# The weights' low parts kept in DRAM between the two token halves

## The chip, the cores and the metric

The kernel runs on one core of a Trainium2 chip. The engines are named as the profile names them: PE is TensorE (matmuls; PEld is its loading of weights), DVE is VectorE, ACT is ScalarE, POOL is GpSimd, and SP (SyncE) issues most DMAs. The metric is the device time of one execution in microseconds (us), the median of several runs.

## The reference

Two layers of a decoder trunk over 1024 tokens of width 1024, in float32. Each layer is

```python
a = rmsnorm(h, norm_mix_pre[i])
u = jnp.einsum('bsd,de->bse', a, w_in[i])
...
mix = jnp.concatenate([y_attn, y_conv, y_pool], axis=-1)
mix = jnp.einsum('bse,ed->bsd', mix, w_out[i])
h = h + rmsnorm(mix, norm_mix_post[i])
m = rmsnorm(h, norm_mlp_pre[i])
m = jnp.square(jax.nn.relu(jnp.einsum('bsd,df->bsf', m, w_up[i])))
m = jnp.einsum('bsf,fd->bsd', m, w_down[i])
h = h + rmsnorm(m, norm_mlp_post[i])
gate = jax.nn.sigmoid(jnp.einsum('bsd,de->bse', h, ple_gate[i]))
h = h + gate * jnp.einsum('bsp,pd->bsd', p[i], ple_proj[i])
```

`y_attn` is an attention in which an indexer picks 256 keys for each query, `y_conv` a causal convolution of 31 taps with a layer norm, `y_pool` a set of trailing means.

## The kernel before

The tokens are cut into two halves of 512. `PHASES` lists what is done in which order, for (layer, half): the input projections of both halves of layer 0, then the long phase "m" (output projection, MLP, gate) of half 0, then the input projection of layer 1 for half 0, and so on. So every weight matrix is used twice: by half 0, and some hundred microseconds later by half 1. The attention and the convolution of a half (`conv_pool`, `attention`) are generators that are advanced beside the dense work, with a budget per phase (`RATES`).

A **unit** is one output block of 128 columns for one token half: eight blocks of 128 rows of a weight matrix times eight slices of the input, into one PSUM bank. Matmuls run on a short float format, so weight and input are each split into a high and a low part, and a unit takes three matmuls for each of the eight blocks (`dense`): high x high, high x low (L248, or L246 where `fresh` is set) and low weight x high input (L249, or L245), 24 in all. A phase "m" has 8 output blocks, 4 half-size units for the layer's extra embedding, 32 up, 32 down and 8 gate units; an input projection has 21.

`prepare` brings the weights of one unit: SP loads the raw block of 512 KB into one of two buffers `wraw` (L199); for each half of it (four row blocks) ACT copies it into the short format, the high part `whi` (L204), and POOL subtracts this from the raw block, which gives the low part `wlo` (L205). `whi` and `wlo` have four half-size buffers each, so two units fit. `weights` calls `prepare` for the next unit just before the matmuls of the present one are written; each half buffer comes free when the matmuls of the half unit that read it are done. Semaphore waits follow from these buffers.

The instructions of each engine are then put in order by a scheduler that simulates the time: it may let matmuls of two or three units take turns where an operand comes late. This happens behind a normalisation (`post_norm`): the eight input slices of the next units are made one after another, by DVE (L867, L266 or L261), POOL (the addition L868) and ACT (L265), and PE has two units, with `fresh` set, work on each slice as it comes. I call such a place a joint.

Of the kernel before, what the change touches and what calls it, by code (L numbers as in the profile page):

```python
# [8 lines left out]
F32 = mybir.dt.float32  # L9
F32R = mybir.dt.float32r  # L10
# [6 lines left out]
OP = mybir.AluOpType  # L17

P = 128
S = 1024  # L20
D = 1024
DEPTH = 2
HALF = 512
NK = D // P
# [22 lines left out]
WIN_ORDER = WIN_ATT + WIN_CONV  # L47


def win_order(l, hf):  # L50

    return WIN_CONV + WIN_ATT if CONV_FIRST[l][hf] else WIN_ORDER
# [34 lines left out]
def tile_trunk(ctx: ExitStack, tc: tile.TileContext, xT, pT, pos, vecs, invf, cinv,  # L87
               win, wout, wup, wdown, wgate, wple, wcp, outT):
    nc = tc.nc
    te, ve, sc, gp, sy = nc.tensor, nc.vector, nc.scalar, nc.gpsimd, nc.sync  # L90
# [5 lines left out]
    dram = ctx.enter_context(tc.tile_pool(name="dram", bufs=1, space=bass.MemoryType.DRAM))  # L96
# [20 lines left out]
    cpS = dram.tile([DEPTH, 512, S], F32, name="cpS")  # L117
    eS = dram.tile([DEPTH, NK, P, S], F32, name="eS")
    tabS = dram.tile([4, P, S], F32, name="tabS")


    slots = Ring("slot", 16, [P, 2, HALF], F32R)
    wraw = Ring("wraw", 2, [P, 8, P])
    whi = Ring("whi", 4, [P, 4, P], F32R)
    wlo = Ring("wlo", 4, [P, 4, P], F32R)
    dtmp = Ring("dtmp", 11, [P, HALF])
    ctmp = Ring("ctmp", 5, [P, HALF])
    cmat = Ring("cmat", 6, [P, HALF], F32R)
# [64 lines left out]
        dtmp.put(*got)  # L193


    def prepare(src):
        n = src.shape[1] // 4
        raw = wraw.get()
        sy.dma_start(raw[:, :4 * n], src)  # L199
        parts = []  # L200
        for i in range(n):
            hi, lo = whi.get(), wlo.get()
            r = raw[:, 4 * i:4 * i + 4]
            sc.activation(hi, r, AF.Copy)  # L204
            gp.tensor_tensor(lo, r, hi.bitcast(F32), op=OP.subtract)  # L205
            parts.append((hi, lo))
        wraw.put(raw)
        return parts


    coming = []
    for l, hf, phase in PHASES:
        if phase == "win":
            coming += [win[l, WIN_ORDER.index(n)] for n in win_order(l, hf)]
        else:
            if (l, hf) == (0, 0):
                coming += [wout[l, o][:, 4:] for o in range(NK)] + [wout[l, o][:, :4] for o in range(NK)]
            else:
                coming += [wout[l, o] for o in range(NK)]
            coming += [wple[l, i] for i in range(2, 4)]  # L220
            for gr in range(4):
                coming += [wup[l, gr * 8 + u] for u in range(8)] + [wdown[l, gr, o] for o in range(NK)]
            coming += [wple[l, i] for i in range(2)] + [wgate[l, o] for o in range(NK)]
    ready = []

    def weights():
        while coming and (not ready or len(ready) <= 1 and len(whi.free) >= 2):
            ready.append(prepare(coming.pop(0)))
        return ready.pop(0)

    def done(parts):
        for hi, lo in parts:
            whi.put(hi)
            wlo.put(lo)

    def pieces(parts):
        return [(hi[:, j], lo[:, j]) for hi, lo in parts for j in range(4)]

    def dense(ps, ws, xs, fresh=False):

# [10 lines left out]
    def unit(xs, fresh=False):  # L251
        ws = weights()
        ps = pd.get()
        dense(ps, pieces(ws), [(x[:, 0], x[:, 1]) for x in xs], fresh)
        done(ws)
        return ps
# [6 lines left out]
    def split_g(hi, lo, src, g):  # L263

        sc.activation(hi, src, AF.Identity, scale=g)  # L265
        ve.scalar_tensor_tensor(lo, src, g, hi.bitcast(F32), op0=OP.mult, op1=OP.subtract)  # L266
# [617 lines left out]
    def embedding(l, hf, pairs, keep):  # L884

        ts = slice(hf * HALF, hf * HALF + HALF)
        pl = [slots.get() for _ in range(2)]
        for c in range(2):
            x = dtmp.get()
            sy.dma_start(x, pT[l, c * P:(c + 1) * P, ts])  # L890
            split(pl[c][:, 0], pl[c][:, 1], x)
            dtmp.put(x)

        def fill():
            for i in pairs:
                w = weights()
                for j in range(2):
                    pp = pd.get()
                    dense(pp, pieces(w)[2 * j:2 * j + 2], [(x[:, 0], x[:, 1]) for x in pl])
                    e = dtmp.get()  # L900
                    sc.activation(e, pp, AF.Copy, scale=0.5)
                    pd.put(pp)
                    if keep is not None:
                        keep.append(e)
                    else:
                        sy.dma_start(eS[l, 2 * i + j, :, ts], e)
                        dtmp.put(e)
                    yield
                done(w)
            slots.put(*pl)  # L910
        return fill
# [117 lines left out]
    def first_x(hf):  # L1029
        ts = slice(hf * HALF, hf * HALF + HALF)  # L1030
        sq = Sq()
        xs = []
        for k in range(NK):
            h = dtmp.get()
            sy.dma_start(h, xT[k * P:(k + 1) * P, ts])
            if k == 0 and hf == 0:
                ready.append(prepare(coming.pop(0)))
            x = slots.get()
            xs.append(x)
            split_g(x[:, 0], x[:, 1], h, vec[:, 0, V_MIX_PRE + k:V_MIX_PRE + k + 1])  # L1040
            sq.add(h)
            dtmp.put(h)
        return xs, sq
# [33 lines left out]
    def drain(l, hf):  # L1077

        while advance([x for x in bg if x[0] == (l, hf)]) is not None:
            pass  # L1080

    state["x", 0, 0] = first_x(0)
    for i, (l, hf, phase) in enumerate(PHASES):
        if phase == "win":
            extra = {}
            if i == 0:
                extra = {2: lambda: (sy.dma_start(fr, invf), rope_tables(0)), 5: lambda: rope_tables(1),
                         16: lambda: state.update({("x", 0, 1): first_x(1)})}
            run(win_phase(l, hf, *state["x", l, hf]), RATES[i], extra)
        else:  # L1090
            drain(l, hf)
            run(m_phase(l, hf), RATES[i])
# [62 lines left out]
```

## Time and profile before

| | us |
|---|---|
| median of three runs | 2885.41 |
| lowest and highest of them | 2882.80, 2891.74 |
| the profiled execution | 2882.24 |
| its span, first to last instruction | 2880.4 |

| engine | busy us | share of the span |
|---|---|---|
| PE | 2736.7 | 95% |
| DVE | 1917.1 | 67% |
| ACT | 1477.3 | 51% |
| POOL | 1468.7 | 51% |

The page gives the busy time of each engine; a view by phase gives the same for stretches of the span, with the TensorE clock that was granted (1.00 is full speed) and the share of time in which the 16 DMA engines moved packets. The views of waits say for each engine after whose instruction it went on. The order of time lists instructions with their start, their length and, in brackets, the idle time of the engine before them and what ended it. A matmul's row is 0.39 us long, but matmuls are pipelined and follow each other more closely; what counts is the distance of their starts. The phases, by their DMAs: input projections of layer 0 from 0 to 150 us (half 0) and to 300 us (half 1); phase "m" of half 0 to 930 us; input projection of layer 1, half 0, to 1190 us (with the gate before it); phase "m" of layer 0, half 1, to 1650 us; input projection of layer 1, half 1, to 1800 us; the phases "m" of layer 1 to 2376 and 2880 us.

### The profile page before, as it was taken

How to read it: one execution, taken by the hardware profiler on the slowest of the kernel's cores; microseconds unless marked ns; L12 is line 12 of the kernel's file. 1: busy time of each engine (PE TensorE's matmuls, PEld its weight loads, DVE VectorE, ACT ScalarE, POOL GpSimd, SP SyncE). 2: the span in 40 equal slices, each digit the busy share in tenths (PEclk: the TensorE clock that was granted, in tenths of full speed). 3: DMA queues.
4: the chain of work that ended last, by engine and by line, in shares of the span. 5: the costliest groups of instructions: out<-in, count | busy, mean ns of one | idle time of the engine just before them, and what ended most of it. 6: DMA issues, size and time to landing. Idle time of an engine off the chain costs nothing.

```text
span 2880.4 us, 37724 instructions
## 1 busy us (share of the span) xinstructions
PE 2736.7 (95%) x12648; PEld 2250.3 (78%) x12648; DVE 1917.1 (67%) x3473; ACT 1477.3 (51%) x2804; POOL 1468.7 (51%) x1161
## 2 busy tenths in 40 slices
PE   7889999999998899999999989999999999999998
PEld 6677877787887677778888767878878878788886
DVE  7989779899768877896312558699996662511123
ACT  5356567774553423675434423677744644533343
POOL 4655435444333766554444775455443346544446
PEclk9999999999998999999999999999999999999999
DMA  5676564332433456633323457544223344432233
GB/s 186 194 194 204 161 154 115 100 101 85 103 94 119 158 160 214 187 116 106 98 98 113 136 181 224 149 123 114 93 87 98 104 147 153 147 103 95 95 110 124
DMA packets 195667, 384.91 MB, mean 134 GB/s; under 512 B 17424, under 2 KB 76944, under 8 KB 195472
## 3 DMA queue, kind: packets, MB, share of 16 engines
q1 hardware_dynamic: 138192, 330.58, 35.1%
q0 software_dynamic: 57280, 51.91, 8.7%
q8 instruction: 100, 1.64, 0.2%
q14 instruction: 95, 0.78, 0.1%
HBM read 307.97 MB, written 74.45 MB: 133 GB/s over the span
## 4 chain that ended last, share of the span: by engine, by line
PE 68%; DVE 17%; DMA 6%; issue 4%; POOL 2%; ACT 2%; SPq 0%; POOLq 0%; ACTq 0%; DVEq 0%
PE pd L243 19%; PE pd L249 19%; PE pd L248 19%; PE bank L591 5%; DVE bank L527 3%; PE bank L781 2%; DVE idx L638 2%; POOL wlo L205 1%; DVE dtmp L261 1%; PE bank L790 1%; PE bank L789 1%; DVE slot L266 1%; DMA wraw<-win 1%; DVE dtmp L867 1%; DMA row<-cpS 1%
## 5 line engine op out<-in xcount | busy, mean ns | idle before, releaser
L205 POOL TENSOR_TENSOR wlo<-wraw,whi 128x512 fp32r<-128x512 f32 x824 | 1130.8, 1378 | 1151.0 <-ACT whi L204 1101.2
L243 PE MATMUL pd<-slot,whi 128*128 128x512 f32 x3296 | 1310.4, 398 | 55.3 <-ACT slot L260 11.5
L248 PE MATMUL pd<-slot,whi 128*128 128x512 f32 x3168 | 1248.1, 394 | 4.3 <-DVE slot L266 3.2
L249 PE MATMUL pd<-slot,wlo 128*128 128x512 f32 x3168 | 1242.6, 394 | 3.7 <-POOL wlo L205 3.4
L204 ACT ACTIVATE whi<-wraw 128x512 fp32r<-128x512 f32 x824 | 511.1, 627 | 717.0 <-PE pd L248 494.1
L243 PEld LDWEIGHTS pd<-slot,whi 128*128 128x128 f32 x3296 | 628.4, 191 | 197.1 <-ACT whi L204 18.8
L249 PEld LDWEIGHTS pd<-slot,wlo 128*128 128x128 f32 x3168 | 601.0, 190 | 129.7 <-POOL wlo L205 7.8
L248 PEld LDWEIGHTS pd<-slot,whi 128*128 128x128 f32 x3168 | 602.0, 190 | 126.7 <-DVE slot L266 5.8
L591 PE MATMUL bank<-kd,qst 128*128 128x512 f32 (+3 forms) x1024 | 249.2, 362 | 24.4 <-DVE mxc L759 10.9
L591 PEld LDWEIGHTS bank<-kd,qst 128*128 128x128 f32 x1024 | 181.6, 193 | 57.5 <-DVE mxc L759 12.8
L969 DVE SCALAR_TENSOR_TENSOR dtmp<-pd,rb 128x512 f32<-128x512 f32 x112 | 76.8, 686 | 199.9 <-PE pd L249 199.9
L985 DVE TENSOR_TENSOR yT<-yT,pd 128x512 f32<-128x512 f32 x96 | 65.7, 685 | 197.2 <-PE pd L249 196.9
L638 DVE SCALAR_TENSOR_TENSOR idx<-row,wiT,idx 128x640 f32<-128x640 f32 (+3 forms) x120 | 164.2, 1369 | 20.0 <-ACT row L632 16.0
L261 DVE TENSOR_TENSOR slot<-dtmp,slot 128x512 fp32r<-128x512 f32 x144 | 118.2, 825 | 72.5 <-ACT slot L260 72.2
L527 DVE SCALAR_TENSOR_TENSOR bank<-row,vec,bank 128x512 f32<-128x512 f32 x232 | 163.4, 745 | 0.6
L632 ACT ACTIVATE row<-bank 128x512 f32<-128x512 f32 (+3 forms) x256 | 120.4, 522 | 51.0 <-PE bank L591 39.0
L661 DVE TENSOR_SCALAR_CACHE_REDUCE row<-row,cc 128x640 f32<-128x640 uint16 (+1 forms) x124 | 133.6, 1077 | 16.5 <-ACT row L675 14.6
L283 DVE TENSOR_TENSOR dtmp<-dtmp,dtmp 128x512 f32<-128x512 f32 x100 | 105.0, 1050 | 50.5 <-ACT dtmp L279 49.5
L675 ACT ACTIVATE row<-row,cc 128x768 f32<-128x768 uint16 (+1 forms) x124 | 121.6, 983 | 25.2 <-DVE cc L681 17.5
L971 ACT ACTIVATE dtmp<-dtmp 128x512 f32<-128x512 f32 x128 | 80.1, 629 | 86.6 <-DVE dtmp L969 84.5
L261 DVE TENSOR_TENSOR cmat<-bank,cmat 128x512 fp32r<-128x512 f32 (+1 forms) x160 | 98.3, 630 | 31.1 <-ACT cmat L260 22.3
L759 DVE CUSTOM_DVE_ANT_0 row<-bank,idx 128x512 f32<-128x512 f32 (+3 forms) x160 | 90.8, 591 | 33.1 <-PE bank L591 28.6
(211 smaller groups left out, 2925.0 us busy)
## 6 DMA issues: line engine op xcount, KB each, us to landing
wraw<-wup SPq DMA_DIRECT2D x128, 512.0 KB, 3.2
wraw<-wdown SPq DMA_DIRECT2D x128, 512.0 KB, 3.2
wraw<-win SPq DMA_DIRECT2D x84, 512.0 KB, 4.1
qiS<-dtmp SPq DMA_DIRECT2D x64, 256.0 KB, 2.5
slot<-mixS POOLq DMA_DIRECT2D x32, 512.0 KB, 7.6
wraw<-wgate SPq DMA_DIRECT2D x32, 512.0 KB, 3.4
qst<-qiS POOLq DMA_DIRECT2D x48, 256.0 KB, 4.4
hS<-yT SPq DMA_DIRECT2D x48, 256.0 KB, 2.4
```

Of the source, the lines that this page charges most:

```text
L204: sc.activation(hi, r, AF.Copy)
L205: gp.tensor_tensor(lo, r, hi.bitcast(F32), op=OP.subtract)
L243: te.matmul(ps, wh, xh, start=i == 0, stop=False)
L248: te.matmul(ps, wh, xl, start=False, stop=False)
L249: te.matmul(ps, wl, xh, start=False, stop=i == n - 1)
L261: ve.tensor_tensor(lo, src, hi.bitcast(F32), op=OP.subtract)
L527: ve.scalar_tensor_tensor(acc[:, c] if k == TAPS - 1 else pa, src, w, pa, op0=OP.mult, op1=OP.add)
L591: te.matmul(ps[:, :n1 - n0], q, kd[:, k, k0 + n0:k0 + n1], start=k == 0, stop=k == 1)
L632: sc.activation(r[:, n0:n1], ps[:, :n1 - n0], AF.Relu)
L638: ve.scalar_tensor_tensor(idx[j], r, w, idx[j], op0=OP.mult, op1=OP.add)
L661: ve.tensor_scalar(flags[:, :Ws[j]], of[j], t, None, op0=op, op1=OP.add, accum_out=dst[:, j:j + 1])
L675: sc.activation(flags[:, :Ws[j]], of[j], AF.Sign, scale=-1.0, bias=c[:, j:j + 1], accum_out=cnt[:, j:j + 1])
```

## The change

When a weight is used first (half 0), its low part is made by POOL as before and then also written to a new DRAM tensor `wloS`, by SP. When it is used again (half 1), SP loads the low part from there, and POOL does nothing for it. The high part is made by ACT both times, from the raw block, which is loaded both times. For the load the low part's ring is changed from four half-size buffers to two whole ones; there are as many bytes as before. `done` gives a whole low buffer back. The list `coming` now carries a key for each weight, by which `prepare` knows whether it has been made.

```diff
+    wloS = dram.tile([105 * DEPTH, P, 8, P], F32, name="wloS")
...
-    wlo = Ring("wlo", 4, [P, 4, P], F32R)
+    wlo = Ring("wlo", 2, [P, 8, P], F32R)
...
-    def prepare(src):
+    known, made = {}, set()
+
+    def prepare(src, key, k0=0):
+
         n = src.shape[1] // 4
-        raw = wraw.get()
+        raw, low = wraw.get(), wlo.get()
         sy.dma_start(raw[:, :4 * n], src)
+        again = (*key, k0) in made
+        made.add((*key, k0))
+        at = wloS[known.setdefault(key, len(known))][:, k0:k0 + 4 * n]
+        if again:
+            sy.dma_start(low[:, :4 * n].bitcast(F32), at)
         parts = []
         for i in range(n):
-            hi, lo = whi.get(), wlo.get()
+            hi, lo = whi.get(), low[:, 4 * i:4 * i + 4]
             r = raw[:, 4 * i:4 * i + 4]
             sc.activation(hi, r, AF.Copy)
-            gp.tensor_tensor(lo, r, hi.bitcast(F32), op=OP.subtract)
+            if not again:
+                gp.tensor_tensor(lo, r, hi.bitcast(F32), op=OP.subtract)
             parts.append((hi, lo))
+        if not again:
+            sy.dma_start(at, low[:, :4 * n].bitcast(F32))
         wraw.put(raw)
-        return parts
+        return parts, low
...
     def done(parts):
-        for hi, lo in parts:
+        for hi, lo in parts[0]:
             whi.put(hi)
-            wlo.put(lo)
+        wlo.put(parts[1])
```

In the program there are now 412 subtractions instead of 824, 218 writes of a low part and 210 loads of one. Lines behind `prepare` have moved by 15: the raw load is L203, the load of a low part L208, the subtraction L215, its write L218, the matmuls are L258, L263 and L264 (fresh: L260 and L261).

Two places show how the order moves. The first is SP's queue at the first up-projections of the last phase (layer 1, half 1): `hS` is the residual that `post_norm` writes, `wraw0`, `wraw1` and `wlo0`, `wlo1` are the two buffers each. Before:

```order
L874 DMA hS_66<-yT_136 128x512 [waits DMAHW4_49,Pool_49]
L199 DMA wraw0_91<-wup 128x1024 [waits DMAHW5_49,Pool_49]
L199 DMA wraw1_92<-wup 128x1024 [waits DMAHW6_49,Pool_49]
L199 DMA wraw0_91<-wup 128x1024 [waits DMAHW7_49,DMAHW5_49,Pool_49]
L199 DMA wraw1_92<-wup 128x1024 [waits DMAHW6_49,DMAHW0_49,Pool_49]
```

and after:

```order
L889 DMA hS_66<-yT_135 128x512 [waits DMAHW1_49,DMAHW0_49,Pool_49]
L208 DMA wlo0_98<-wloS_75 128x1024 [waits PE_49]
L208 DMA wlo1_99<-wloS_75 128x1024 [waits DMAHW2_49,PE_49]
L203 DMA wraw0_92<-wup 128x1024 [waits DMAHW3_49,Activation_49]
L203 DMA wraw1_93<-wup 128x1024 [waits DMAHW4_49,Activation_49]
L208 DMA wlo0_98<-wloS_75 128x1024 [waits DMAHW5_49,DMAHW1_49,PE_49]
L203 DMA wraw0_92<-wup 128x1024 [waits DMAHW6_49,DMAHW3_49,Activation_49]
```

The loads of low parts stand behind the writes of the residual, each waits for PE, and from there on a low and a raw load take turns; the raw load waits for ACT where it waited for POOL.

The second place is PE at the same joint. `pd0`, `pd1` and `pd2` are PSUM banks, one for each unit in work, `slot6` to `slot13` the eight input slices; the units on `pd1` and `pd2` are the first two up-projections, the one on `pd0` is the third. Before:

```order
L243 MATMUL pd0_137<-slot6_81,whi2_95 128x512 [waits DVE_49,Activation_49]
L248 MATMUL pd0_137<-slot6_81,whi2_95 128x512
L243 MATMUL pd1_138<-slot11_86,whi3_96 128x512 [waits Activation_49]
...
L249 MATMUL pd0_137<-slot6_81,wlo2_99 128x512 [waits Pool_49]
...
L249 MATMUL pd0_137<-slot9_84,wlo2_99 128x512
L246 MATMUL pd1_138<-slot11_86,whi3_96 128x512 [waits DVE_49]
...
L246 MATMUL pd1_138<-slot13_88,whi3_96 128x512 [waits DVE_49]
L246 MATMUL pd2_139<-slot13_88,whi1_94 128x512
```

and after:

```order
L261 MATMUL pd1_137<-slot13_89,whi3_97 128x512 [waits DVE_49]
L261 MATMUL pd2_138<-slot13_89,whi1_95 128x512
L258 MATMUL pd1_137<-slot6_82,whi0_94 128x512 [waits Activation_49]
L263 MATMUL pd1_137<-slot6_82,whi0_94 128x512
L264 MATMUL pd0_136<-slot6_82,wlo0_98 128x512 [waits DMAHW1_49]
L258 MATMUL pd0_136<-slot7_83,whi2_96 128x512
```

Twelve matmuls of the third unit stood among those of the first two; now only its first two (ahead of these rows) do, and the first that reads its low part stands behind the end of both and waits for a DMA.

## Rows read from the trace of the kernel before

**Rows 1.** The page, part 1: each engine's busy time, share, instructions

```profile
PE 2736.7 (95%) x12648; PEld 2250.3 (78%) x12648; DVE 1917.1 (67%) x3473; ACT 1477.3 (51%) x2804; POOL 1468.7 (51%) x1161
```

**Rows 2.** Busy times by phase: engines (instructions), PE clock, DMA share, GB/s

```profile
0.00:150.00 150.00, 120.73 (x490) 94.46 (x490) 126.72 (x179) 67.67 (x111) 79.78 (x68) 0.94 0.60 193
...
150.00:300.00 150.00, 141.96 (x664) 116.77 (x664) 134.24 (x371) 89.12 (x204) 85.13 (x75) 0.97 0.68 195
...
1190.00:1650.00 460.00, 450.24 (x2084) 371.35 (x2083) 241.70 (x567) 232.27 (x459) 237.36 (x184) 1.00 0.39 119
...
1650.00:1800.00 150.00, 135.71 (x593) 108.94 (x592) 105.67 (x132) 48.82 (x85) 96.51 (x79) 0.97 0.65 202
...
2376.00:2880.00 504.00, 492.65 (x2171) 402.94 (x2169) 139.47 (x166) 195.37 (x327) 273.13 (x205) 0.99 0.36 118
```

**Rows 3.** The page, part 5: the subtraction that makes a low part

```profile
L205 POOL TENSOR_TENSOR wlo<-wraw,whi 128x512 fp32r<-128x512 f32 x824 | 1130.8, 1378 | 1151.0 <-ACT whi L204 1101.2
```

**Rows 4.** What PE waited for: total us, times, longest

```profile
PE pd L249 <- POOL wlo L205: 3.4, 5, 1.2
```

**Rows 5.** Order of time, a dense stretch: start, us, instruction

```profile
1501.01 0.39 PE L249 MATMUL pd<-slot,wlo 128*128 128x512 f32 x1
...
1501.44 0.69 DVE L985 TENSOR_TENSOR yT<-yT,pd 128x512 f32<-128x512 f32 x1 [4.75 <-PE pd L249]
...
1501.98 1.30 POOL L205 TENSOR_TENSOR wlo<-wraw,whi 128x512 fp32r<-128x512 f32 x1 [1.44 <-ACT whi L204]
...
1503.30 5.77 SPq L199 DMA_DIRECT2D wraw<-wup  x2
...
1506.88 0.69 DVE L985 TENSOR_TENSOR yT<-yT,pd 128x512 f32<-128x512 f32 x1 [4.75 <-PE pd L249]
```

**Rows 6.** Landing of raw loads in 150:300, 1190:1650, 1650:1800, 2376:2880

```profile
DMA to landing us min/median/max: 3.2/3.7/4.7
DMA to landing us min/median/max: 3.1/3.3/5.4
DMA to landing us min/median/max: 3.2/3.7/6.5
DMA to landing us min/median/max: 2.5/3.2/5.9
```

**Rows 7.** Order of time on PE at the joint of 2461 us

```profile
2461.07 0.50 PE L243 MATMUL pd<-slot,whi 128*128 128x512 f32 x1 [1.64 <-ACT slot L265]
...
2470.95 0.48 PE L243 MATMUL pd<-slot,whi 128*128 128x512 f32 x1
...
2472.61 0.49 PE L249 MATMUL pd<-slot,wlo 128*128 128x512 f32 x1
...
2474.79 0.39 PE L249 MATMUL pd<-slot,wlo 128*128 128x512 f32 x1
...
2475.02 0.62 PE L246 MATMUL pd<-slot,whi 128*128 128x512 f32 x2
...
2477.74 0.61 PE L246 MATMUL pd<-slot,whi 128*128 128x512 f32 x2
```

**Rows 8.** The same joint on POOL

```profile
2471.25 1.30 POOL L205 TENSOR_TENSOR wlo<-wraw,whi 128x512 fp32r<-128x512 f32 x1
...
2472.51 1.76 POOL L868 TENSOR_TENSOR yT<-dtmp,dtmp 128x512 f32<-128x512 f32 x1
...
2474.23 1.74 POOL L205 TENSOR_TENSOR wlo<-wraw,whi 128x512 fp32r<-128x512 f32 x1
```

**Rows 9.** Busy times of 4 us behind that wait, with the granted clock

```profile
2462.00:2466.00 4.00, 3.75 (x11) 2.59 (x10) 4.00 (x6) 1.29 (x2) 2.79 (x2) 0.57 0.79 240
```

**Rows 10.** The chain of waits: one raw load in the first second-use phase

```profile
175.55 8.00 DMA wraw<-win
```

**Rows 11.** Order of time on DVE at the same joint

```profile
2461.73 0.74 DVE L266 SCALAR_TENSOR_TENSOR slot<-yT,vec,slot 128x512 fp32r<-128x512 f32 x1
...
2471.38 3.44 DVE L266 SCALAR_TENSOR_TENSOR slot<-yT,vec,slot 128x512 fp32r<-128x512 f32 x2 [0.57 <-ACT slot L265]
```

More of the change, by code (lines that the diff above doesn't have):

```diff
@@ L213, in tile_trunk @@
         if phase == "win":
-            coming += [win[l, WIN_ORDER.index(n)] for n in win_order(l, hf)]
+            coming += [(win[l, WIN_ORDER.index(n)], ("win", l, n)) for n in win_order(l, hf)]
         else:
             if (l, hf) == (0, 0):
-                coming += [wout[l, o][:, 4:] for o in range(NK)] + [wout[l, o][:, :4] for o in range(NK)]
-            else:
-                coming += [wout[l, o] for o in range(NK)]
-            coming += [wple[l, i] for i in range(2, 4)]
+                coming += [(wout[l, o][:, 4:], ("out", l, o), 4) for o in range(NK)]
+                coming += [(wout[l, o][:, :4], ("out", l, o)) for o in range(NK)]
+            else:
+                coming += [(wout[l, o], ("out", l, o)) for o in range(NK)]
+            coming += [(wple[l, i], ("ple", l, i)) for i in range(2, 4)]
             for gr in range(4):
-                coming += [wup[l, gr * 8 + u] for u in range(8)] + [wdown[l, gr, o] for o in range(NK)]
-            coming += [wple[l, i] for i in range(2)] + [wgate[l, o] for o in range(NK)]
+                coming += [(wup[l, gr * 8 + u], ("up", l, gr, u)) for u in range(8)]
+                coming += [(wdown[l, gr, o], ("down", l, gr, o)) for o in range(NK)]
+            coming += [(wple[l, i], ("ple", l, i)) for i in range(2)]
+            coming += [(wgate[l, o], ("gate", l, o)) for o in range(NK)]
     ready = []
@@ L227, in weights @@
         while coming and (not ready or len(ready) <= 1 and len(whi.free) >= 2):
-            ready.append(prepare(coming.pop(0)))
+            ready.append(prepare(*coming.pop(0)))
         return ready.pop(0)
     def done(parts):
-        for hi, lo in parts:
+        for hi, lo in parts[0]:
             whi.put(hi)
-            wlo.put(lo)
+        wlo.put(parts[1])
     def pieces(parts):
-        return [(hi[:, j], lo[:, j]) for hi, lo in parts for j in range(4)]
+        return [(hi[:, j], lo[:, j]) for hi, lo in parts[0] for j in range(4)]
     def dense(ps, ws, xs, fresh=False):
@@ L1036, in first_x @@
             if k == 0 and hf == 0:
-                ready.append(prepare(coming.pop(0)))
+                ready.append(prepare(*coming.pop(0)))
             x = slots.get()
```

## The prediction

> **What bounds the kernel now.** I read the page's busy times first, then the busy times by phase, then what TensorE waits for, and last the order of time at the places that the change touches. TensorE is busy for 95% of the span [rows 1], so nothing can be won but the 144 us in which it is idle. I call the phases of the second token half, in which the weights come for the second time, the second-use phases: the two projections (150 to 300 us and 1650 to 1800 us) and the two long phases of output projection, MLP and gate (1190 to 1650 us and 2376 to 2880 us). TensorE is idle there for 8.0, 14.3, 9.8 and 11.4 us [rows 2], 43.4 us in all. That is the most that a change of the second use alone can give back, apart from the clock.
>
> POOL is not what TensorE waits for. The 824 subtractions that make the low parts take 1378 ns each, and POOL stood idle before them for 1151 us, nearly all of it until ACT had made the high part [rows 3]. TensorE waited for a low part 5 times, 3.4 us in all [rows 4]. In the order of time of a dense stretch the reader sees why: a unit of 24 matmuls takes 5.44 us (1501.44 to 1506.88), and POOL has a half of the low part ready 1.8 us after the previous unit ended, 3.6 us before that unit begins [rows 5].
>
> **What is removed.** 412 of 824 subtractions, 412 x 1.378 = 568 us of POOL's time [rows 3], beside TensorE's work throughout. What of it lay on the path: the waits for a low part (at most 3.4 us over both halves, [rows 4]), and what the subtractions cost others. They sit between POOL's additions at the joint described below, 1.30 and 1.74 us [rows 8], which I count there. And VectorE is slower beside them: line 266 takes 0.74 us at one place and 1.7 us each at another, where POOL is busy throughout [rows 11]. Outside the joints VectorE keeps TensorE waiting for a part of the 43.4 us only; I take 6 us off, with 0 and 20 us (nearly half of 43.4) as ends.
>
> **What is added in the second use.** 210 loads of a low part, 512 KB nearly all, each on SP's queue. Buffer and order matter more than the bytes. A low part now has one of two whole buffers, so the load for unit n+2 waits until the last matmul of unit n has read it, where a subtraction needed a half buffer and waited for a half unit. SP works in order, so the raw load for n+3, and whatever result is to be written, stands behind that wait; a raw load has 5 us and more to spare, since its unit starts two units later.
>
> In a dense stretch the load still fits. The buffer is free 0.43 us after the last matmul of unit n began (1501.01 to 1501.44, [rows 5]). The first matmul that reads the new low part stands 27 places later, 27 x 0.227 = 6.1 us. That leaves 5.7 us for a landing that takes 3.3 us in the median and 5.9 us at worst in the long phases [rows 6]. I cost this at nothing for some 150 units; the cover is the 24 matmuls of unit n+1, and without it each load would show its 3.3 us.
>
> Where two units run together there is no such cover. Behind each normalisation (four joints in the second-use phases: before the first up-projections and before the gates, in both long phases) the first two units take turns, because their inputs come one by one. At 2461 us the trace shows it: TensorE waits 1.64 us for the first input, and while the later inputs are being made it runs 12 matmuls of the third unit, from 2470.95 to 2474.79; the first two units end with the pair at 2477.74 [rows 7]. The third unit could start since its low part, in half buffers, was made early. In the changed order its low part is asked for when the first unit ends, and only three matmuls stand between. Per joint:
> - The inputs come sooner, as two subtractions leave POOL's row of additions: up to 1.30 + 1.74 = 3.0 us [rows 8], of which I take 1.7 (the second stands behind the last addition). Ends 0 and 3.0.
> - The landing is on the path: 0.1 us for the waits and 4.2 us, between the median of 3.2 and the worst of 5.9 us in that phase [rows 6], above the median because the writes of the residual are just ahead.
> - 44 matmuls of units three and four are left then instead of 36: 8 x 0.227 = 1.8 us.
> - A wait of this size costs clock. After the 1.64 us wait the granted clock fell to 0.57 over 2462 to 2466 us, the lower level (1.2 GHz) for most of it [rows 9]: 4 x 0.43 = 1.7 us more. A second wait follows the first here, so I count it once more.
>
> That is -1.7 + 4.3 + 1.8 + 1.7 = 6.1 us, four times 24 us. The ends are -3.0 + 3.3 + 1.8 = 2.1 us without a fall of the clock, 8 us in all, and 6.0 + 1.8 + 3.4 = 11.2 us with twice the fall, 45 us in all.
>
> The two projection phases are the other place. The DMA engines are busy there for 0.68 and 0.65 of the time at 195 and 202 GB/s [rows 2]. 21 loads of 524 kB in 150 us are 73 GB/s more; by the long phases (0.36 at 118 GB/s, [rows 2]) each 100 GB/s costs 0.3 of the engines, so they come to about 0.9. A unit lasts 150 / 21 = 7.1 us there, so a load has some 7 us. Landings are 3.7 us in the median and 6.5 at worst [rows 6], and the chain of waits goes through one raw load of 8.00 us [rows 10]. I let one unit in four come 1 us late: 42 / 4 = 10 us. Ends 0 and 42 us (each unit 1 us late).
>
> The Trainium skill (DMA: Bandwidth & Descriptors, Specifications) puts the HBM limit of a core at about 358 GB/s. By that the phases would stand at 275 / 358 = 0.77 at most after the change, the lateness would be near 0 and the sum 10 us lower. I go by the busy share of the rows, which counts the small packets too.
>
> **What is added in the first use.** 218 writes of a low part. They wait for POOL, as the raw loads did, and nobody waits for their landing but a subtraction two units on. Half buffers remain half buffers there, and the joints of the first half keep their order. The first projection's engines go from 0.60 [rows 2] to about 0.8. I take 4 us, ends 0 and 20 (one 5 us landing late in each of four places).
>
> **The sum.** 24 + 10 - 6 + 4 = 32 us on the profiled execution's 2882.24 us (span 2880.4 and 1.8 around it) gives 2914 us. That execution lies 3 us below the median of the runs, 2885.41 us; I leave the forecast at 2914.
>
> **The rivals.** *Faster by VectorE.* The mechanism is the lock between VectorE and POOL: with no subtraction in the second half VectorE's operations with two inputs no longer stand behind one. For it: line 266, 0.74 against 1.7 us [rows 11]. Against it: TensorE is idle for 43.4 us there and waits mostly for other things. If each joint gained its 3.0 us (12 us), the 6 us outside grew to 12 and the low parts landed in time after all, it would be 2882 - 24 + 10 = 2868 us. It decides where a landing at a joint is covered by work I have not counted. The Trainium skill (SBUF — State Buffer, Who interferes with whom) says that the port pair the two share is held for a whole instruction; by that rule each such meeting is worth a full subtraction, which is the case for this rival.
>
> *No change.* The joints cost their lower end, 8 us, no projection unit is late, and the relief takes it back: 2882 + 8 - 6 + 1 = 2885 us.
>
> *Much slower: the dense stretches lose their cover.* If the raw load issued right behind holds the low part up, so that landings go from 3.3 to more than 5.7 us, each of some 150 dense units is late. At 0.5 us each that is 75 us on top: 2990 us. For it: landings of 5.4 and 5.9 us exist [rows 6]. Against it: one low and one raw load each 5.44 us bring the engines to some 0.65 only, by the shares above.
>
> That the change doesn't do what it says is excluded by the order of instructions: 210 loads stand on SP's queue and 412 subtractions are left.
>
> **How the numbers follow.** The forecast (joints and projections, 2895 to 2955 us) has 0.60, the faster rival 0.12, no change 0.18, the dense stretches 0.10. A measurement of this kernel tells 0.3% (8.7 us) from no change. Faster 0.12, same 0.18, slower 0.70. The range leaves out the dense case (0.10), half of the faster rival and 0.04 of the forecast's upper end: 2872 to 2955 us.
>
> **What would show it.** In the changed profile: TensorE waits of 2 to 5 us at the third unit of four joints, ended by the DMA of a low part, with a fall of the granted clock behind each; no such wait in 1300 to 1600 us; POOL's busy time down by about 568 us; DMA share near 0.9 in the second projections. It would be wrong if TensorE waited for low parts in the dense stretches, or if the joints showed no wait because the loads landed under the turns of the first two units.

## The result and the profile after

The changed kernel takes 2912.4 us (median of four runs, 2906.9 to 2912.9), the kernel before 2884.1 us in the same runs. The ratio is 1.0092, with a 95% interval of 1.0065 to 1.0119: slower by some 27 us, against a forecast of 2914 us. The profiled execution took 2906.9 us, with a span of 2905.1.

The page of the changed kernel, part 1, answers to [rows 1], its part 5 to [rows 3]:

```profile
PE 2747.7 (95%) x12648; PEld 2254.7 (78%) x12648; DVE 1833.1 (63%) x3473; ACT 1477.2 (51%) x2804; POOL 916.2 (32%) x749
...
L215 POOL TENSOR_TENSOR wlo<-wraw,whi 128x512 fp32r<-128x512 f32 x412 | 581.1, 1419 | 670.5 <-ACT whi L213 571.2
```

POOL lost 412 subtractions and 552 us, VectorE 84 us without losing an instruction, and TensorE is busy 11 us longer with the same instructions, at a mean granted clock of 0.976 against 0.980. The busy times by phase answer to [rows 2] (columns as there: engines, granted clock, DMA share, GB/s; the last phase begins later now):

```profile
150.00:300.00 150.00, 143.33 (x672) 118.91 (x673) 119.95 (x366) 87.80 (x201) 28.94 (x35) 0.97 0.89 270
1190.00:1650.00 460.00, 449.07 (x2066) 370.78 (x2065) 218.83 (x572) 233.69 (x463) 40.81 (x38) 0.99 0.61 200
1650.00:1800.00 150.00, 140.68 (x609) 112.37 (x608) 89.34 (x132) 52.53 (x89) 34.26 (x33) 0.97 0.86 279
2400.00:2880.00 480.00, 465.27 (x2041) 379.32 (x2041) 114.26 (x159) 186.71 (x312) 43.03 (x32) 0.99 0.61 209
```

In the two second-use projections (first and third line) the DMA share went from 0.68 and 0.65 to 0.89 and 0.86, and yet TensorE's idle time fell, from 8.0 to 6.7 us and from 14.3 to 9.3. In the third line 132 VectorE instructions took 89.3 us; in the same stretch before, 132 that are nearly the same took 105.7. The difference lies in those with both inputs in SBUF (though one group of four among them became longer). Here are two groups of that stretch, each before and after (instructions, busy us, mean ns); the first takes one input from a PSUM bank, the second both from SBUF:

```profile
L527 DVE SCALAR_TENSOR_TENSOR bank<-row,vec,bank 128x512 f32<-128x512 f32 x58 | 40.6, 746 | 0.1
L542 DVE SCALAR_TENSOR_TENSOR bank<-row,vec,bank 128x512 f32<-128x512 f32 x58 | 40.4, 747 | 0.1
...
L261 DVE TENSOR_TENSOR dtmp<-dtmp,dtmp 128x512 fp32r<-128x512 f32 x11 | 11.2, 1021 | 0.2 <-ACT dtmp L260 0.2
L276 DVE TENSOR_TENSOR dtmp<-dtmp,dtmp 128x512 fp32r<-128x512 f32 x10 | 6.8, 691 | 4.2 <-ACT whi L213 3.1 <-ACT dtmp L275 1.0
```

What TensorE waited for answers to [rows 4] (total us, times, longest):

```profile
PE pd L264 <- DMA wlo<-wloS: 18.8, 16, 4.1
PE pd L260 <- DMA wlo<-wloS: 7.7, 4, 3.4
PE pd L264 <- POOL wlo L215: 3.6, 7, 1.2
```

L264 is the low-part matmul of an ordinary unit, L260 that of the units that take turns. The same view of 1300 to 1600 us is empty: the dense stretches kept their cover. In the projections the low parts held TensorE up for 2.8 us (150 to 320 us) and 6.2 us (1650 to 1811 us); the rest, 17.5 us, lies in the long phases.

The order of time on TensorE at the joint that [rows 7] showed before:

```profile
2475.12 0.50 PE L258 MATMUL pd<-slot,whi 128*128 128x512 f32 x1 [1.64 <-ACT slot L280]
2477.36 0.50 PE L260 MATMUL pd<-slot,wlo 128*128 128x512 f32 x1 [1.74 <-DMA wlo<-wloS]
2477.69 0.39 PE L258 MATMUL pd<-slot,whi 128*128 128x512 f32 x1
2477.92 0.40 PE L261 MATMUL pd<-slot,whi 128*128 128x512 f32 x1
2480.42 0.80 PE L260 MATMUL pd<-slot,wlo 128*128 128x512 f32 x1 [2.10 <-DMA wlo<-wloS]
...
2495.12 0.40 PE L263 MATMUL pd<-slot,whi 128*128 128x512 f32 x1
2496.72 0.50 PE L264 MATMUL pd<-slot,wlo 128*128 128x512 f32 x1 [1.21 <-DMA wlo<-wloS]
```

and on SP's queue, which issues the loads (idle time is not shown for a queue):

```profile
2468.11 2.82 SPq L879 DMA_DIRECT2D dtmp<-hS  x3
2471.03 0.38 SPq L208 DMA_DIRECT2D wlo<-wloS  x1
2471.50 0.86 SPq L921 DMA_DIRECT2D eS<-dtmp  x2
2473.51 0.32 SPq L208 DMA_DIRECT2D wlo<-wloS  x1
...
2493.42 0.80 SPq L208 DMA_DIRECT2D wlo<-wloS  x2
```

The third unit waits as forecast (1.21 us, for a load issued at 2493.42). The first two wait as well (1.74 and 2.10 us). The first load left at 2471.03, behind three loads of `hS` on the queue. The second left at 2473.51; the queue was free a microsecond earlier, but the unit ahead gave back its whole low buffer only with its last matmul, and the load then took long, as the chain of waits shows (start, us, what):

```profile
2473.24 0.25 PE pd L264
2473.51 6.87 DMA wlo<-wloS
2480.42 0.80 PE pd L260
```

And the clock falls behind it, to 0.50 or 1.2 GHz:

```profile
2479.00:2485.00 6.00, 4.58 (x11) 3.61 (x12) 5.18 (x7) 3.00 (x5) 5.70 (x5) 0.50 0.89 254
```

For a ledger I cut both traces at the same work, at the starts of TensorE's matmuls number 504, 1008, 2976, 3480, 5448, 5952 and 7920 among those with a prepared weight. Before, these stand at 176.2, 324.0, 986.0, 1142.3, 1657.0, 1802.9 and 2407.5 us, after at 172.8, 319.9, 993.4, 1148.0, 1668.3, 1810.6 and 2420.5 us. By these cuts the first long phase of the second use begins at 1142 us in the kernel before, not at 1190 as in the stretches above.

| phases | before, us | after, us | difference | forecast |
|---|---|---|---|---|
| projections, first use | 332.4 | 327.4 | -5.0 | +4 for both first uses |
| long phases, first use | 1266.7 | 1283.3 | +16.6 | (in the +4) |
| projections, second use | 293.7 | 289.5 | -4.2 | +10 |
| long phases, second use | 987.6 | 1005.0 | +17.4 | +24 |
| relief of VectorE and POOL | | | (in the above) | -6 |
| span | 2880.4 | 2905.1 | +24.7 | +32 |

So the sum held, while its terms did not: the joints were taken too large, the projections on the wrong side, and the first use too small.

### The profile page after: what moved, and what is told of

It is laid out like the page before. It is cut to its first block, busy times and chain, and to the rows that moved or that the text cites. A ratio compares the mean times of both kernels' runs of the same rounds, so it can differ in the third digit from the quotient of the medians.

```text
span 2905.1 us, 37877 instructions
## 1 busy us (share of the span) xinstructions
PE 2747.7 (95%) x12648; PEld 2254.7 (78%) x12648; DVE 1833.1 (63%) x3473; ACT 1477.2 (51%) x2804; POOL 916.2 (32%) x749
## 4 chain that ended last, share of the span: by engine, by line
PE 70%; DVE 12%; DMA 10%; issue 3%; ACT 2%; POOL 2%; SPq 1%; POOLq 0%; ACTq 0%; DVEq 0%
PE pd L258 20%; PE pd L264 19%; PE pd L263 19%; PE bank L606 5%; DMA wlo<-wloS 3%; DVE bank L542 2%; PE bank L796 2%; POOL wlo L215 1%; PE bank L804 1%; PE bank L805 1%; DMA qst<-qiS 1%; DVE slot L276 1%; DMA wraw<-wdown 1%; PE pd L261 1%; DMA wraw<-win 1%
## 5 line engine op out<-in xcount | busy, mean ns | idle before, releaser
L258 PE MATMUL pd<-slot,whi 128*128 128x512 f32 x3296 | 1315.5, 400 | 47.5 <-ACT whi L213 16.5
L264 PE MATMUL pd<-slot,wlo 128*128 128x512 f32 x3168 | 1245.6, 396 | 23.0 <-DMA wlo<-wloS 18.8
L263 PE MATMUL pd<-slot,whi 128*128 128x512 f32 x3168 | 1248.9, 395 | 3.1 <-DVE slot L281 3.1
L215 POOL TENSOR_TENSOR wlo<-wraw,whi 128x512 fp32r<-128x512 f32 x412 | 581.1, 1419 | 670.5 <-ACT whi L213 571.2
L258 PEld LDWEIGHTS pd<-slot,whi 128*128 128x128 f32 x3296 | 630.0, 191 | 189.0 <-ACT whi L213 23.6
L264 PEld LDWEIGHTS pd<-slot,wlo 128*128 128x128 f32 x3168 | 602.2, 190 | 158.5 <-DMA wlo<-wloS 27.2
L263 PEld LDWEIGHTS pd<-slot,whi 128*128 128x128 f32 x3168 | 603.5, 190 | 124.8 <-DVE slot L281 5.1
L323 POOL TENSOR_TENSOR rrn<-rvn,mhalf 128x4 f32<-128x4 f32 x8 | 8.4, 1051 | 634.7 <-DVE rvn L321 634.7
L276 DVE TENSOR_TENSOR slot<-dtmp,slot 128x512 fp32r<-128x512 f32 x144 | 111.8, 780 | 78.1 <-ACT slot L275 78.0
L690 ACT ACTIVATE row<-row,cc 128x768 f32<-128x768 uint16 (+1 forms) x124 | 121.5, 982 | 21.9 <-DVE cc L696 15.9
L298 DVE TENSOR_TENSOR dtmp<-dtmp,dtmp 128x512 f32<-128x512 f32 x100 | 83.3, 833 | 67.5 <-ACT dtmp L294 67.0
```

Of the source, the lines that this page charges most:

```text
L258: te.matmul(ps, wh, xh, start=i == 0, stop=False)
L263: te.matmul(ps, wh, xl, start=False, stop=False)
L264: te.matmul(ps, wl, xh, start=False, stop=i == n - 1)
L276: ve.tensor_tensor(lo, src, hi.bitcast(F32), op=OP.subtract)
L690: sc.activation(flags[:, :Ws[j]], of[j], AF.Sign, scale=-1.0, bias=c[:, j:j + 1], accum_out=cnt[:, j:j + 1])
```

## The experiments

Diffs are against the changed kernel, unless another is named. "Idle" is a window's length less TensorE's busy time in it. A single profile can lie 8 us off its kernel's median (e1_rings), so the verdicts rest on the ratios, and on idle times and the ledger's cuts where several kernels agree.

**The low ring and the joints.**

```diff
 e1_rings:
-        again = (*key, k0) in made
+        again = False
-        if not again:
-            sy.dma_start(at, low[:, :4 * n].bitcast(F32))
 e8_joints:
+        seen = (*key, k0) in made
+        joint = key[0] == "gate" and key[2] < 4 or key[0] == "up" and key[2] == 0 and key[3] < 4
+        again = seen and not joint
...
-        if not again:
+        if not seen:
 e5_halves:
-            sy.dma_start(low[:, :4 * n].bitcast(F32), at)
+            for i in range(n):
+                sy.dma_start(low[:, 4 * i:4 * i + 4].bitcast(F32), at[:, 4 * i:4 * i + 4])
```

> The low parts are made by POOL in both halves, as before; only the rings keep the changed shape (two whole low buffers instead of four halves). Theory A (the joints' read-back costs some 20 us, the writes of the first half 5 to 10): 2884 us, within 6 of the kernel before. Theory B (the two whole buffers and the order of instructions that follows from them cost it, whoever fills them): 2905 to 2915 us. Theory C (the added DMA bytes cost it, wherever they fall): 2884 us.

Measured: 2881.0 us, ratio 1.0006 (0.9995 to 1.0018). Two whole low buffers cost nothing by themselves.

> The changed kernel, but the first four up-projections and the first four gates of each second-use phase make their low parts on POOL again (16 of 210 units), so no joint waits for a load. Theory A: the waits for low parts at the joints (16 us) and the clock lost behind them (up to 7 us) go, 2889 to 2896 us. Theories B and C: 2910 us or more, since rings and nearly all bytes stay.

Measured: 2910.1 us, ratio 1.0099 (1.0086 to 1.0112). Nothing came back. The order of time shows why: at three of the four joints the wait moved to the first unit that reads again. In the last gate phase it now stands at the fifth unit:

```profile
2874.78 0.50 PE L260 MATMUL pd<-slot,whi 128*128 128x512 f32 x1 [2.21 <-ACT whi L215]
...
2876.07 0.80 PE L266 MATMUL pd<-slot,wlo 128*128 128x512 f32 x1 [0.53 <-DMA wlo<-wloS]
```

Here the first wait ends with the high part, whose raw load stood on SP's queue too. So with whole buffers the exposed load belongs to the change from subtracting or taking turns to reading, not to the joint's units as such. With half loads that change need not cost: e16_skip below begins to read behind the first up-projections, and no matmul waits there.

> The changed kernel, but each read-back is two loads of 256 KB, each waiting for its half buffer only, as the subtractions did. Theory A: at a joint the first half can be asked for while the last inputs are made, so about half of the joints' loss goes, 2898 to 2904 us, or nothing if the second load stands on the path as the whole one did. Theory C: as many bytes, 2912 us.

Measured: 2894.5 us, ratio 1.0048 (1.0035 to 1.0061). Half of the loss is gone, some 13 us, with the same bytes. A half load waits for a half buffer, as a subtraction did. In the last phase TensorE waited for low parts for 3.0 us, all of it at units in turns; in the changed kernel it was 10.2:

```profile
PE pd L261 <- DMA wlo<-wloS: 3.0, 2, 2.8
```

The cuts of the ledger put the gain where the loads are read. These are differences from the kernel before, in us (e16_skip follows below):

| | changed | e5_halves | e16_skip |
|---|---|---|---|
| projections, first use | -5.0 | -5.0 | -4.6 |
| long phases, first use | +16.6 | +23.3 | +15.9 |
| projections, second use | -4.2 | -14.8 | -15.4 |
| long phases, second use | +17.4 | +4.4 | -0.4 |

**Writes without reads, reads without writes.**

```diff
 e2_writes:
-        again = (*key, k0) in made
+        again = False
+        first = (*key, k0) not in made
-        if not again:
+        if first:
 e3_reads:
-        at = wloS[known.setdefault(key, len(known))][:, k0:k0 + 4 * n]
+        idx = known.setdefault(key, len(known))
+        at = wloS[idx % 8][:, k0:k0 + 4 * n]
-        if not again:
+        if not again and idx < 8:
 e9_tiny (against e2_writes):
-            sy.dma_start(at, low[:, :4 * n].bitcast(F32))
+            sy.dma_start(at[:, :1, :4], low[:, :1, :4].bitcast(F32))
```

> The first half writes its low parts to DRAM, but nobody reads them back: POOL makes them again in the second half. Theory A: 2884 plus 4 to 11, 2888 to 2895 us. Theory B: 2905 to 2915 us. Theory C: half of the bytes, half of the loss, 2898 us.

Measured: 2910.0 us, ratio 1.0095 (1.0082 to 1.0108). The writes alone seemed to be the whole loss, against the theory that I had put on record.

> The changed kernel without nearly all its writes: only the first 8 weights write their low part, and every load in the second token half takes one of these 8 blocks (so the low parts of all but 8 weights are those of another weight); number, size and place of the loads are as in the changed kernel. So far the writes with nobody reading (e2_writes) cost 29 us, as much as the whole change, and the two whole buffers (e1_rings) nothing. Theory E (bytes of the writes: they share the DMA engines with loads that are waited for, and the read-back is neutral, its waits paid back by the subtractions that are gone): 2875 to 2890 us. Theory A as put on record (the joints pay for the read-back): 2900 us or more. Theory D (order: any added DMA makes the scheduler put the attention in another order, and that order loses the time): 2895 us or more, since the loads change the order too.

Measured: ratio 1.0042 (1.0028 to 1.0056), some 12 us; median 2899.2 us. The reads cost something too, though less than A wanted, and the two parts add up to some 39 us where the change costs 27.

> e2_writes with its 218 writes in their places on SP's queue, each waiting for POOL as before, but each of 2 KB (16 bytes of each partition) instead of 512 KB; nothing reads them, POOL subtracts both times. Theory E (bytes): back to 2880 to 2886 us. Theory F (the write as an entry of SP's queue, its wait and the semaphore work, whatever its size): 2900 to 2912 us, as e2_writes.

Measured: 2890.2 us, ratio 1.0026 (1.0014 to 1.0038). The 218 entries on the queue, with the order that comes with them, cost some 7 us. What e2_writes loses beyond that goes with the bytes or with its own order; the next two runs bear on which.

**The writes in two halves.**

```diff
 e12_mw (against e2_writes):
+        first = key[0] != "win" and (*key, k0) not in made
 e15_ww (against e2_writes):
+        first = key[0] == "win" and (*key, k0) not in made
```

> e2_writes with the writes of the two input projections left out: only the 176 writes of the first-use long phases (87 MB) are left; nothing reads them, POOL subtracts both times. In the profile of e2_writes the long phases of the first half were 14.2 and 8.9 us longer than before, the layer-0 projection of the second half 12.4 us longer though it holds no write, and the order of TensorE's instructions there differs from that of before by some places; here that order is again that of before up to 320 us. Theory E (bytes beside the attention's loads): 2897 to 2908 us, most of the loss of e2_writes. Theory D (the loss comes with the changed order in the projections): 2880 to 2892 us.

Measured: 2912.4 us, ratio 1.0102 (1.0083 to 1.0121).

> The other half of e2_writes: only the 42 writes of the two input projections (22 MB), nobody reads, POOL subtracts both times. The order in the projections is that of e2_writes. Theory E by bytes alone: 22 of 109 MB, 2883 to 2890 us. Theory D (order), or a loss that sits in the projections because their DMA engines are the busiest: 2893 to 2905 us.

Measured: 2905.1 us, ratio 1.0077 (1.0065 to 1.0089). Each half alone costs nearly as much as both: these costs do not add. In the trace of e15_ww 15.8 us of its loss lie in the layer-0 projection of the second half, where it writes nothing; e2_writes lost 12.4 us there, and the changed kernel, whose POOL is free there, gained 0.7. What e2_writes waited for in that phase (172 to 332 us) was POOL and the attention:

```profile
PE pd L265 <- POOL wlo L216: 3.6, 4, 2.5
PE bank L607 <- DMA qst<-qiS: 3.1, 1, 3.1
PE bank L607 <- DVE mxc L775: 3.0, 3, 1.7
```

TensorE's matmuls stand in another order there than before (the attention and the norms have up to 28 matmuls fewer done at the same matmul with a prepared weight), the same in e2_writes and e15_ww. In e9_tiny and e12_mw, whose order there is that of before, this phase lost 1.0 and 0.0 us. So e2_writes does not measure a part of the change: some 12 us of it are a loss that the change does not have. That the order makes them fits these four kernels, but the order was never changed by itself, and another order need not lose: the changed kernel's differs by up to 44 matmuls there.

The long phases of the first use are another matter. They are 24.2 us longer in e12_mw, which writes there, and 6.8 us in e15_ww, which does not. By the same cuts they are 12.6 to 24.2 us longer than before in the six kernels that write all their low parts there (mean 19.2), and 2.3 to 10.3 us in the six others that write none or tiny ones (mean 6.5). So the writes, with the order that they bring, cost some 13 us there.

**Where the bytes of the writes hurt.**

```diff
 e10_late:
+        while len(pending) > (0 if (*key, k0) in made else 1):
+            sy.dma_start(*pending.pop(0))
...
-            sy.dma_start(at, low[:, :4 * n].bitcast(F32))
+            pending.append((at, low[:, :4 * n].bitcast(F32)))
 e16_skip (against e5_halves):
-        again = (*key, k0) in made
+        kept = key[0] not in ("out", "ple") and key[:3:2] != ("up", 0)
+        again = kept and (*key, k0) in made
-        if not again:
+        if kept and not again:
```

> The changed kernel with each write put behind the raw load of the unit two further on, instead of ahead of it, so that the raw load does not share the engines with the write issued just before it (on SP's queue it now goes raw n+2, write n; the subtraction that reuses the buffer waits for the write). Bytes and loads are unchanged. Theory E in its narrow form (the write delays the raw load right behind it): 2885 to 2900 us. E in its wide form (the bytes delay the attention's loads): 2905 to 2915 us, as the changed kernel.

Measured: 2901.9 us, ratio 1.0052 (1.0039 to 1.0065). It is 10 us better than the changed kernel, though the two intervals touch, but no stretch shows where: its profiled execution, the longest of its five runs, is only 2 us shorter than the changed kernel's, the shortest of four. Between 330 and 520 us the raw up-projections land in 4.9 us instead of 6.9, as wanted, and TensorE is idle for 19.5 us there against 20.3. So the raw loads are not what it waits for in that stretch. What the 10 us are stays open.

> e5_halves (read-back in two half loads) without keeping the low parts of the units that run beside the attention at the start of each long phase: the output projection, the extra embedding and the first group of up-projections are subtracted both times; 170 of 218 writes are left, 21 of them in each first-use projection as before. In the changed kernel the layer-0 long phase of the first half is 11 us longer and the layer-1 one 5 us, and most of it falls into the first 200 us, where those units run. Theory E in its last form (writes beside the attention's loads): 8 to 12 us less than e5_halves (2894.5 us), 2882 to 2887 us. If it is the order of the attention's instructions and not the writes beside them, which stays nearly that of e5_halves here: 2891 to 2897 us.

Measured: 2881.1 us, ratio 0.9996 (0.9987 to 1.0004). The total is that of the kernel before again, 15 us less than e5_halves, with 170 of the 218 writes still made. The busy times of 330 to 520 us, where the attention of layer 0 runs beside the output projection and the first up-projections, in the changed kernel and in e16_skip:

```profile
330.00:520.00 190.00, 169.72 (x793) 137.63 (x792) 153.81 (x218) 124.55 (x265) 82.50 (x70) 0.95 0.61 168
```

```profile
330.00:520.00 190.00, 175.62 (x833) 142.89 (x832) 160.64 (x233) 128.26 (x269) 87.87 (x75) 0.96 0.54 137
```

TensorE was idle for 20.3 us beside 168 GB/s, and for 14.4 us beside 137. Over all kernels of this study:

| | idle 330 to 520 us | GB/s there |
|---|---|---|
| writes in it: changed, e2, e5, e8, e10, e12 | 20.3, 21.5, 20.4, 16.6, 19.5, 23.0 | 164 to 176 |
| none, or tiny ones: before, e1, e3, e7, e9, e13, e15, e16 | 14.9, 16.1, 16.2, 12.8, 15.3, 15.1, 16.3, 14.4 | 131 to 137 |

The means are 20.2 and 15.1 us. How far one profile can be off is seen in e8_joints: up to 1100 us it has the instructions of the changed kernel in the same order, and yet 16.6 against 20.3. In that stretch of the changed kernel the longest waits are those for the attention's own loads:

```profile
PE bank L606 <- DMA qst<-qiS: 5.8, 3, 2.6
```

Their median landing is 5.9 us, before 4.3. In e16_skip the same wait is 3.3 us, before 1.4. Over the kernels of the table these waits are 2.4 to 5.8 us (mean 4.5) with writes and 1.4 to 3.9 (mean 2.8) without, so they are a part of the 5 us only. These 5 us are a third of the 15 that e16_skip won.

Two things limit what e16_skip shows. The order is not held: in 324 to 502 us (by the time before) its matmuls stand in the order of e7_winhalf, not, as I had expected, nearly in that of e5_halves. That the writes and not the order make the 5 us is argued from the many orders on either side of the table. And the loss did not go where it arose. By the table under e5_halves the long phases of the first use, without the writes beside the attention, are 7.4 us shorter than in e5_halves, but still 15.9 us longer than before, about as in the changed kernel. Another 4.8 us went in the long phases of the second use, whose first joints read nothing now. What brings the total back to that of before is the projections, which are 20.0 us shorter than before.

**Only the projections kept.** The aim was a version that beats both.

```diff
 e7_winhalf (against e5_halves):
+        kept = key[0] == "win"
+        again = again and kept
-        if not again:
+        if kept and not again:
 e13_win4 (the same, with the low ring of the kernel before):
+            half = at[:, 4 * i:4 * i + 4]
+            if again:
+                sy.dma_start(lo.bitcast(F32), half)
...
+                if kept:
+                    sy.dma_start(half, lo.bitcast(F32))
```

> Low parts kept and read back for the two input projections only (42 of 210 weights), as two loads of 256 KB each; all other weights are subtracted both times. In the profile of e5_halves the two first-use projections were 1.5 and 3.5 us shorter than before and the two second-use ones 2.9 and 11.9 us shorter, while the long phases were 13 to 24 us longer in the first half. Theory E with the loss in the long phases of the first half: 2862 to 2876 us, faster than the kernel before. Theory D (order): 2890 to 2910 us. Theory A with late projections (its second term): 2885 to 2900 us.

Measured: 2881.4 us, ratio 0.9990 (0.9979 to 1.0002).

> Low parts kept for the projections only, as in e7_winhalf, but with the low ring of the kernel before (four half-size buffers) and each half written and read by itself (256 KB), so that a read waits for the half unit that held its buffer and the subtractions of all other weights stand as before. e7_winhalf gave 0.999 of before: its four projections were 21 us shorter and its long phases 18 us longer though nothing is kept there. If the whole low buffers and what they do to the order are what the long phases pay for: 2862 to 2874 us. If the long phases pay whatever the buffers (theory D, the order): 2878 to 2890 us.

Measured: 2889.6 us, ratio 1.0021 (1.0012 to 1.0031). The gain in the four projections is there in both traces (21 and 11 us by the cuts of the ledger), and both give it back in the long phases (18 and 10 us), where they hold no added transfer. The half-size buffers, the reason for e13_win4, do not help. What gives it back is open. No version beat the kernel before by more than its interval.

## Why the prediction was right, and where it was not

- **Sum.** 2914 us against 2912.4, by errors that cancel.
- **Joints, 24 us (8 to 45).** The mechanism was there: the third unit of each of the four joints waited for its low part (1.4, 1.5, 1.2 and 4.1 us), and half loads, which undo just this, won 13.0 us in these phases. The clock fell behind that wait at three of the joints (0.57, 0.59 and 0.63 over 4 us), and at the one shown behind the first two units' waits. The landing term was put at four times 4.3, or 17.2 us, and the low parts did hold TensorE up for 17.5 us in the long phases, but less than half of it was at the third unit. What I had missed are the loads of the first two units (7.7 us in four waits): three of the four left only when the unit ahead gave back its whole buffer, and three took 6.3 to 6.9 us until the matmul could start, where I had put 4.2. The term itself was too large: these phases grew by 17.4 us, with drift in it, since e1_rings, which reads nothing, shows 3.1 us there.
- **Projections, +10 us (0 to 42): the step that failed.** The lateness was sized well (9.0 us of waits, DMA share 0.89 and 0.86 against the forecast 0.9), but the phases became 4.2 us shorter. The relief, put at 6 us over all of the second use, falls into these two phases. Waits of 9.0 us and a net of -4.2 make it 13 us there alone, if nothing else moved. That fits e5_halves and e16_skip: with half loads the two phases are 14.8 and 15.4 us shorter than before.
- **First use, +4 us (0 to 20).** The range holds the net 11.6 us of the ledger, the value does not: the long phases alone grew by 16.6 us. I had written that nobody waits for the landing of a write but a subtraction two units on; no wait of TensorE in the trace ends with one. But over all kernels the writes, with the order that they bring, cost some 13 us in these phases. Of this the stretch beside the attention shows 5 us, partly as waits for the attention's loads; the rest is open. The forecast counted on an unchanged order at the joints of the first half; the order of the attention beside the dense work did change.
- **Dense stretches, 0.** Right: no wait for a low part between 1300 and 1600 us, and the largest landing of a raw load in 1190 to 1650 us is 5.5 us.
- **The rivals.** The faster one had its mechanism (132 VectorE instructions of one stretch, 105.7 to 89.3 us) but not the size. That the difference lies in those with both inputs in SBUF, and not in those with one in PSUM, agrees with the Trainium skill (SBUF — State Buffer, Who interferes with whom), by which a VectorE instruction with two SBUF inputs and a GpSimd one that reads SBUF shut each other out for whole instructions. Its bandwidth limit of 358 GB/s (DMA: Bandwidth & Descriptors, Specifications) gives an estimate of 0.75 for the 270 GB/s that were moved; the trace has 0.89, so the busy share of the rows was the better guide.

## What to carry to other kernels

A value that is read back instead of being made again needs the same grain of buffer as the instruction it replaces (half loads won 13 us here), and the place to cost it is where units take turns or wait for inputs, not the steady stretch. Count the added bytes of the *other* half as well: kernels that write in the long phases, with no matmul waiting for it, are some 13 us longer there than kernels that do not, though the order differs too. Half loads, and no writes beside the attention, brought the total back to that of before, but by a gain in other phases; compare the phases before a total is put down to a cause. Where a scheduler orders the work, the parts of a change measured alone need not add up, so see also that the order is the same before a difference is put down to the part.

## What the runs showed of the hardware

- A 512 KB load of an up-projection landed in 3.2 us in the median at 134 GB/s over the whole span, in 4.4 us at 207 GB/s, long before the DMA engines were full (share 0.6 in the long phases). A write of 2 KB took 1.4 us in the median (e9_tiny).
- Over one stretch of 150 us, 132 VectorE instructions became 15% shorter when POOL's subtractions beside them went. The largest case: one subtraction of 16x512 lasted 6.13 us before (from 1720.27 us), beside POOL instructions that followed each other without a gap; after, it took 0.69 us.
